# Gate and up products of a decoder trunk: scales read three steps behind POOL's maximum, second buffers for two tiles, the tanh put behind the third copy

## The chip, the cores and the metric

The kernel runs on one core of one Trainium2 chip. The metric is the device time of one execution in microseconds (us), the median of several runs. The profile comes from one more execution, recorded by the hardware profiler. Engines: PE (TensorE, matmuls; PEld is its weight load), DVE (VectorE), ACT (ScalarE), POOL (GpSimd) and SP (SyncE, which here issues the DMAs). Every engine works its instructions off in order.

## What is computed

One layer of a decoder trunk for a prompt of 2048 positions and eight short sequences of four positions: a mixer (pooling and a state space model, gated), then a feed-forward block, then a norm. The change lies in the first half of the feed-forward block:

```python
hn = _rmsnorm(h, norm_ffn[l])
f = jax.nn.silu(jnp.einsum('btd,df->btf', hn, ffn_w_gate[l])) * jnp.einsum('btd,df->btf', hn, ffn_w_up[l])
h = h + jnp.einsum('btf,fd->btd', f, ffn_w_down[l]).astype(h.dtype)
```

`hn` has 2080 rows of 1024, `ffn_w_gate` and `ffn_w_up` are 1024 x 2816, `ffn_w_down` is 2816 x 1024.

## The kernel before, in words

**Blocks and parts.** Gate and up are computed together for blocks of 128 of the 2816 hidden columns: 22 blocks (`NF`). For each block, `up` runs four parts, one for each range `r` of columns of the input (`XR`: 256, 256, 256 and 272 wide), in the order 1, 2, 3, 0. So the first part of a block is `r` = 1, the third (`r` = 3) is the wide one, the fourth is `r` = 0. Blocks 0 to 19 stand in a section whose order on PE, DVE, ACT and POOL is that of the code (`manual_schedule(engines=IN_ORDER)`); what stands ahead of it, the last two blocks and SP's queue are ordered by the scheduler.

**One part.** The two products are made from seven smaller ones (a Strassen-like scheme over two halves of the depth, gate and up). Each small product is 12 matmuls (four depth slices, three combinations of high and low half-precision parts). `part` adds them up in PSUM banks `x`, `y` and `z`, and uses one bank for several partial sums, so PE must wait until ACT has copied a bank out before it adds the next product: `p1` (line 870) is copied after the first product, `p5` (873) after the second, `u` (876) after the third, `v` (882) after the fifth. The order on PE is products 1, 5, 6, 3, 7, 2, 4. DVE forms the up gate's input `g` = `u` + `y` (its tile is called `w1`, `w` in the profile). `gate` is two ACT instructions: a tanh (855) and a scaling (856); the first `gate` writes `t2` (`t` in the profile), the second writes `t1`, whose tile has the name `u`. POOL adds `p5` += `v` (883) and stores `t2` * `p5` (861, and 864 for the 16 additional columns of the third part); DVE adds `p1` += `z`, makes `t1` * `p1` and stores the other half (861).

All temporary tiles come from the pool `ftmp` with one buffer for each name.

**The work between.** Next to the products, the weights of the next block are converted (`prep(i + 1)`): `hi` is ACT's half-precision conversion with a power-of-two scale, `lo` is DVE's remainder, and DVE makes four sums in tiles `cmb`. The weights of the block after that are loaded (`load(i + 2)`: `gr` and `ur`, `wdrow`: a `cmb` tile) and their scales are made (`stat`): DVE reduces the three tiles to maxima, POOL takes the maximum over the 128 partitions (`partition_all_reduce`, line 746), DVE makes the scales from it (749 to 761, in every second block also `pair`, to 772). This side work is a generator; each `yield` ends a step, and `tick` runs one step at each of four places in every part, so a block has 16 steps. Step 1 stands ahead of the first part's products.

**Out of the stage.** `flush` sends a finished pair of ranges to `f_d` by DMA; then `down` follows.

Of the kernel before, what the change touches and what calls it, by code (L numbers as in the profile page):

```python
# [9 lines left out]
F32 = mybir.dt.float32  # L10
# [687 lines left out]
class FFN:  # L698
# [40 lines left out]
    def stat(self, i, d):  # L739

        E, nc = self.E, self.E.nc
        m = E.small.tile([128, 6], F32, tag="fm", name="fm")
        for j, t in enumerate((*(t.rearrange("p k f -> p (k f)") for t in self.R[i]), d)):
            nc.vector.tensor_reduce(m[:, j:j + 1], t, axis=AX.X, op=OP.max, apply_absolute_value=True)
            yield
        nc.gpsimd.partition_all_reduce(m[:, 3:6], m[:, 0:3], 128, RMAX)
        yield
        b = E.small.tile([128, 4], F32, tag="fb", name="fb")
        nc.vector.tensor_copy(b[:, 0:3], m[:, 3:6])
        nc.vector.tensor_scalar(m[:, 0:2], m[:, 3:5], self.kf, None, op0=OP.mult)  # L750
        tt(E, b[:, 3:4], m[:, 0:1], m[:, 1:2], OP.mult)
        s, inv = pow2(E, b, 4, "pf", 2.0 ** -48, 1e18)
        yield

        c = E.small.tile([128, 8], F32, tag="fc", name="fc")
        nc.vector.tensor_scalar(c[:, 0:2], s[:, 0:2], 0.25, None, op0=OP.mult)
        tt(E, c[:, 2:3], s[:, 0:1], inv[:, 1:2], OP.mult)
        nc.vector.tensor_scalar(c[:, 3:4], c[:, 2:3], -1.0, None, op0=OP.mult)
        nc.vector.tensor_scalar(c[:, 6:8], inv[:, 0:2], self.inv_hn, 4.0, op0=OP.mult, op1=OP.mult)
        nc.vector.tensor_scalar(c[:, 4:5], c[:, 6:7], 0.5, None, op0=OP.mult)  # L760
        nc.vector.tensor_scalar(self.st[:, :, i], s[:, 2:4], 0.25, None, op0=OP.mult)
        self.C[i] = c
# [11 lines left out]
    def prep(self, i):  # L774

        E, nc, c = self.E, self.E.nc, self.C[i]
        g, u = self.R.pop(i)
        f = "p k f -> p (k f)"
        a11, a12, a21, a22 = (t[:, k:k + 4].rearrange(f) for t in (g, u) for k in (0, 4))
        W = self.wp.tile([128, 2, 7, 512], F16, name="W")  # L780
        self.W[i] = W
        S = [self.cmb().rearrange("p (j n) -> p j n", j=2) for j in range(2)]
        s1, s2, s3, s4 = (t[:, j] for t in S for j in range(2))
        src = {0: (slice(0, 2), g.rearrange(f), c[:, 0:1]), 3: (slice(3, 5), S[0].rearrange(f), c[:, 1:2]),
               5: (slice(5, 7), S[1].rearrange(f), c[:, 1:2]), 2: (slice(2, 3), a22, c[:, 1:2])}

        def hi(k):
            o, x, s = src[k]
            nc.scalar.activation(W[:, 0, o].rearrange(f), x, AF.Copy, scale=s)

        def lo(k):
            o, x, s = src[k]
            o = [W[:, v, o].rearrange(f) for v in range(2)]
            nc.vector.scalar_tensor_tensor(o[1], x, s, o[0], op0=OP.mult, op1=OP.subtract)

        hi(0)
        tt(E, s1, a21, a22, OP.add)
        nc.vector.scalar_tensor_tensor(s2, a11, c[:, 3:4], s1, op0=OP.mult, op1=OP.add)
        yield
        hi(3)  # L800
        lo(0)
        yield
        nc.vector.scalar_tensor_tensor(s3, a11, c[:, 2:3], a21, op0=OP.mult, op1=OP.subtract)
        nc.vector.scalar_tensor_tensor(s4, a12, c[:, 2:3], s2, op0=OP.mult, op1=OP.subtract)
        hi(2)
        yield
        hi(5)
        lo(3)
        yield
        lo(5)  # L810
        yield
        lo(2)

    def work(self, i):

        yield from self.prep(i + 1)
        if i + 2 < NF:
            self.load(i + 2)
            d = self.wdrow(i + 2)
            yield  # L820
            yield
            yield
            yield
            yield from self.stat(i + 2, d)
            if i % 2:
                self.pair(i + 1)
        yield
# [5 lines left out]
    def part(self, i, r, first):  # L833


        E, nc, tmp = self.E, self.E.nc, self.tmp
        W, c, X = self.W[i], self.C[i], self.X[r]
        w = XR[r][1]
        F = self.F[i % 2][r // 2]
        T = lambda nm: tmp.tile([128, 272], F32, name=nm)[:, :w]  # L840
        bank = lambda: (self.px.tile([128, 512], F32, name="pa", bufs=2) if first else
                        self.ps.tile([128, 512], F32, name="p", bufs=6))[:, :w]

        def mm(q, p, begin, end):
            a, b = self.P[p]
            for k in range(4):
                ka = slice(k * 128, k * 128 + 128)
                for v, (x, y) in enumerate(((0, 0), (0, 1), (1, 0))):
                    nc.tensor.matmul(q, W[:, x, a, ka], X[b][:, y, k, :w], start=begin and k == v == 0,  # L849
                                     stop=end and k == 3 and v == 2, skip_group_check=True)  # L850

        def gate(g, nm):

            t = T(nm)
            nc.scalar.activation(t, g, AF.Tanh, scale=c[:, 4:5])  # L855
            nc.scalar.activation(t, t, AF.Identity, scale=c[:, 5:6], bias=c[:, 5:6])
            return t

        def store(eng, hf, t, u):
            o = (r % 2) * 2  # L860
            eng.tensor_tensor(F[:, o:o + 2, hf], t[:, :256].rearrange("p (b n) -> p b n", b=2),  # L861
                              u[:, :256].rearrange("p (b n) -> p b n", b=2), op=OP.mult)
            if w > 256:
                eng.tensor_tensor(self.fs[:, i, hf], t[:, 256:], u[:, 256:], op=OP.mult)

        p1, p5, u, v, g = (T(x) for x in ("p1", "p5", "u", "v", "w1"))
        x = bank()
        self.tick()
        mm(x, 1, True, False)
        nc.scalar.copy(p1, x)  # L870
        y = bank()
        mm(y, 5, True, False)
        nc.scalar.copy(p5, y)  # L873
        self.tick()
        mm(x, 6, False, False)
        nc.scalar.copy(u, x)
        mm(y, 3, False, True)
        tt(E, g, u, y, OP.add)
        t2 = gate(g, "t2")
        self.tick()  # L880
        mm(x, 7, False, False)
        nc.scalar.copy(v, x)  # L882
        nc.gpsimd.tensor_tensor(p5, v, p5, op=OP.add)  # L883
        tt(E, t2, t2, g, OP.mult)
        store(nc.gpsimd, 1, t2, p5)
        z = bank()
        mm(z, 2, True, True)
        tt(E, p1, p1, z, OP.add)
        t1 = gate(p1, "u")
        self.tick()  # L890
        mm(x, 4, False, True)
        tt(E, t1, t1, p1, OP.mult)
        store(nc.vector, 0, t1, x)
# [6 lines left out]
    def up(self, ctx, cf, X, F):  # L900
# [9 lines left out]
        for j, src in enumerate(self.x_d):  # L910
            t = xp.tile([128, 2, 4, 256], F16, name=f"x0{j}")
            nc.sync.dma_start(t, src)
            X[0].append(t)
        self.load(1)
        self.ps = pool(cf, "fps", 2, space=PSUM)
        n = NF - 2
        with E.tc.manual_schedule(engines=IN_ORDER):
# [792 lines left out]
```

## Time and profile before

| | |
|---|---|
| median of 3 runs | 2493.27 us (2491.67 to 2493.64) |
| the profiled execution's own time | 2488.81 us |
| its span, first to last instruction | 2487.0 us |
| mean granted TensorE clock | 0.981 |
| busy: PE, PEld, DVE, ACT, POOL | 93%, 65%, 67%, 41%, 18% of the span |
| gate and up stage | from about 1120 to 2039 us |

A share of busy time is a mean over stages with different limits; PE at 93% still has idle time, and the rows below say where and for whom it waited. The ends of matmuls are modelled, since they are pipelined: the record of one lasts longer than the distance to the next. So distances between starts are the surer measure.

### The profile page before, as it was taken

What the parts mean: (1) busy time and instruction counts of PE and PEld (TensorE: products, weight loads), DVE (VectorE), ACT (ScalarE), POOL (GpSimd) and SP (SyncE); (2) the same over time, 40 slices, a digit from 0 to 9 for tenths busy, and PEclk for the clock granted to TensorE, in tenths of its full rate; (3) what the DMA queues carried; (4) which work ended last, traced back from release to release, by engine and by line L of the source; (5) the groups of instructions that cost most, each with busy time, mean ns of one, the idle gap of its engine ahead of it and who ended that gap; (6) DMA issues with size and microseconds to landing.
All of it is one profiled execution on the core that took longest, in us unless ns stands there. A gap on an engine that the chain in (4) does not pass through costs nothing. (4 is left out here: it accounts for less than half of the span.)

```text
span 2487.0 us, 43168 instructions
## 1 busy us (share of the span) xinstructions
PE 2303.8 (93%) x16939; PEld 1611.4 (65%) x16939; DVE 1655.2 (67%) x3866; ACT 1020.6 (41%) x1808; POOL 446.0 (18%) x443
## 2 busy tenths in 40 slices
PE   5869999999999999998999999999999899998998
PEld 4745565654578874556878787878788774443443
DVE  7526795747568778786555555455555678789787
ACT  6422332323444424455444444444444453234332
POOL 3300000000000000001222122121212234445342
PEclk9889999999999999999999999999999999999999
DMA  6224234344434453313212122121212244444332
GB/s 219 64 51 115 70 83 104 83 130 165 149 115 124 116 149 140 120 56 120 77 56 73 61 70 74 62 69 60 77 52 77 85 145 152 144 164 153 128 121 76
DMA packets 209777, 258.03 MB, mean 104 GB/s; under 512 B 33046, under 2 KB 170582, under 8 KB 209053
## 3 DMA queue, kind: packets, MB, share of 16 engines
q1 hardware_dynamic: 209397, 254.83, 32.6%
q8 instruction: 132, 2.16, 0.4%
q14 instruction: 72, 0.59, 0.1%
q10 hardware_dynamic: 144, 0.26, 0.0%
q0 software_dynamic: 32, 0.18, 0.0%
HBM read 167.56 MB, written 86.67 MB: 102 GB/s over the span
## 5 line engine op out<-in xcount | busy, mean ns | idle before, releaser
L849 PEld LDWEIGHTS <-W 128*128 128x128 f16 x7392 | 726.4, 98 | 181.3 <-issue 80.5
L849 PE MATMUL p<-m,W 128*128 128x256 f16 (+1 forms) x3084 | 357.0, 275 | 1.9 <-ACT v L882 1.9
L114 PE MATMUL mm<-xl,wh 128*128 128x512 f16 (+4 forms) x1072 | 347.9, 326 | 7.8 <-DVE xl L136 7.8
L113 PE MATMUL mm<-xh,wh 128*128 128x512 f16 (+4 forms) x1072 | 348.4, 326 | 1.7 <-ACT xh L136 1.6
L115 PE MATMUL mm<-xh,wl 128*128 128x512 f16 (+4 forms) x1072 | 347.7, 326 | 1.6 <-DVE wl L53 1.6
L113 PE MATMUL pd<-m,W 128*128 128x512 f16 x616 | 235.5, 382 | 17.8 <-DVE xr L1096 6.5
L849 PE MATMUL p<-x,W 128*128 128x256 f16 x1848 | 210.6, 274 | 30.8 <-ACT v L882 28.2
L849 PE MATMUL p<-xq,W 128*128 128x256 f16 x1764 | 207.2, 276 | 32.0 <-ACT p L873 28.4
L114 PE MATMUL pd<-m,W 128*128 128x512 f16 x616 | 235.4, 382 | 0.0
L115 PE MATMUL pd<-m,W 128*128 128x512 f16 x616 | 234.7, 382 | 0.5 <-DVE W L307 0.5
L883 POOL TENSOR_TENSOR p<-v,p 128x256 f32<-128x256 f32 (+1 forms) x88 | 71.3, 810 | 750.8 <-ACT v L882 604.3
L115 PEld LDWEIGHTS <-wl 128*128 128x128 f16 x1072 | 107.3, 100 | 76.5 <-issue 9.6
L114 PEld LDWEIGHTS <-wh 128*128 128x128 f16 x1072 | 107.1, 100 | 67.6 <-issue 2.6
L113 PEld LDWEIGHTS <-wh 128*128 128x128 f16 x1072 | 107.0, 100 | 64.7 <-issue 0.3
L307 DVE TENSOR_TENSOR w<-u,p 128x272 f32<-128x272 f32 (+1 forms) x86 | 36.3, 422 | 153.6 <-PE p L849 153.6
L1095 POOL TENSOR_TENSOR xq<-xq,xr 128x512 f32<-128x512 f32 x90 | 128.2, 1444 | 40.7 <-DVE xq L1096 16.0
L114 PEld LDWEIGHTS <-W 128*128 128x128 f16 x616 | 60.6, 98 | 92.2 <-issue 22.0
L115 PEld LDWEIGHTS <-W 128*128 128x128 f16 x616 | 60.7, 99 | 74.8 <-issue 2.4
L113 PEld LDWEIGHTS <-W 128*128 128x128 f16 x616 | 60.6, 98 | 73.7 <-issue 2.1
L855 ACT ACTIVATE t<-w,fc 128x256 f32<-128x256 f32 (+1 forms) x88 | 45.0, 511 | 152.3 <-DVE w L307 152.3
L292 ACT ACTIVATE go<-mm,wc 128x512 f32<-128x512 f32 (+1 forms) x80 | 47.6, 603 | 141.4 <-PE mm L115 113.9
L861 POOL TENSOR_TENSOR m<-t,p 128x256 f32<-128x256 f32 x88 | 97.3, 1106 | 9.0 <-POOL p L883 1.1
(472 smaller groups left out, 4440.3 us busy)
## 6 DMA issues: line engine op xcount, KB each, us to landing
f_d<-m SPq DMA_DIRECT2D x44, 512.0 KB, 2.9
xq<-f_d SPq DMA_DIRECT2D x40, 512.0 KB, 4.6
x<-in_x_prompt_dram SPq DMA_DIRECT2D x32, 512.0 KB, 4.7
xq<-h_d SPq DMA_DIRECT2D x32, 512.0 KB, 4.3
g<-g_d SPq DMA_DIRECT2D x56, 256.0 KB, 2.8
g_d<-go SPq DMA_DIRECT2D x48, 256.0 KB, 2.9
gr<-in_ffn_w_gate_dram SPq DMA_DIRECT2D x23, 512.0 KB, 3.9
ur<-in_ffn_w_up_dram SPq DMA_DIRECT2D x23, 512.0 KB, 3.9
```

The lines of the kernel that those rows point to most:

```text
L113: nc.tensor.matmul(q, ah, bh, start=first, stop=False)
L114: nc.tensor.matmul(q, ah, bl, start=False, stop=False)
L115: nc.tensor.matmul(q, al, bh, start=False, stop=last)
L292: nc.scalar.activation(o[:, :w], q[:, :w], AF.Tanh, scale=cc[:, 1:2])
L307: E.nc.vector.tensor_tensor(o, a, b, op=op)
L849: nc.tensor.matmul(q, W[:, x, a, ka], X[b][:, y, k, :w], start=begin and k == v == 0, stop=end and k == 3 and v == 2, skip_group_check=True)
L855: nc.scalar.activation(t, g, AF.Tanh, scale=c[:, 4:5])
L861: eng.tensor_tensor(F[:, o:o + 2, hf], t[:, :256].rearrange("p (b n) -> p b n", b=2), u[:, :256].rearrange("p (b n) -> p b n", b=2), op=OP ...
L883: nc.gpsimd.tensor_tensor(p5, v, p5, op=OP.add)
L1095: add = (lambda o, x: tt(E, o, o, x, OP.add)) if end else (lambda o, x: nc.gpsimd.tensor_tensor(o, o, x, op=OP.add))
```

## The change

It has four parts.

1. In `stat`, two empty steps stand between POOL's maximum and the instructions that read it, so that they come three steps after it and not one. In `prep` and `work` steps move to make room: `load(i + 2)` is issued by `prep` at its fourth step, `lo(2)` moves up to that step and `lo(3)` and `lo(5)` one step back, and an empty step goes. The block still has 16 steps.
2. The tiles `p5` and `t2` come from a new pool `ftm2` with two buffers for each name.
3. The first `gate` (the tanh and scaling that make `t2`) stands behind the copy of `v` and POOL's addition, and `t2` * `g` and POOL's store stand behind the addition of `z`.
4. The load for block 1 is issued in `prep(0)`; the pool `ftm2` is made after the tiles `x0`.

```diff
 def stat(self, i, d):
         nc.gpsimd.partition_all_reduce(m[:, 3:6], m[:, 0:3], 128, RMAX)
         yield
+        yield
+        yield
         b = E.small.tile([128, 4], F32, tag="fb", name="fb")
...
 def prep(self, i):
         hi(2)
         yield
+        lo(2)
         hi(5)
+        if i + 1 < NF:
+            self.load(i + 1)
+        yield
         lo(3)
         yield
         lo(5)
-        yield
-        lo(2)
 
     def work(self, i):
         yield from self.prep(i + 1)
         if i + 2 < NF:
-            self.load(i + 2)
             d = self.wdrow(i + 2)
-            yield
             yield
             yield
             yield
...
 def part(self, i, r, first):
-        T = lambda nm: tmp.tile([128, 272], F32, name=nm)[:, :w]
+        T = lambda nm: (self.tm2 if nm in ("p5", "t2") else tmp).tile([128, 272], F32, name=nm)[:, :w]
...
         tt(E, g, u, y, OP.add)
-        t2 = gate(g, "t2")
         self.tick()
         mm(x, 7, False, False)
         nc.scalar.copy(v, x)
         nc.gpsimd.tensor_tensor(p5, v, p5, op=OP.add)
-        tt(E, t2, t2, g, OP.mult)
-        store(nc.gpsimd, 1, t2, p5)
+        t2 = gate(g, "t2")
         z = bank()
         mm(z, 2, True, True)
         tt(E, p1, p1, z, OP.add)
+        tt(E, t2, t2, g, OP.mult)
+        store(nc.gpsimd, 1, t2, p5)
         t1 = gate(p1, "u")
...
 def up(self, ctx, cf, X, F):
-        self.load(1)
+        self.tm2 = pool(cf, "ftm2", 2)
         self.ps = pool(cf, "fps", 2, space=PSUM)
```

The order on the engines changes with it. (Lines of the changed kernel are one or two higher.) First DVE in the fourth part of a block, from the reading of the maximum (`fb<-fm`); `w` is `g`, `t` is `t2`, `p` is `p1` or a PSUM bank, `fc` and `fst` are the scales. Before:

```order
L749 COPY fb<-fm 128x3
L750 TENSOR_SCALAR fm<-fm,gmf 128x2
L307 TENSOR_TENSOR fb<-fm 128x1
L44 TENSOR_SCALAR pw<-fb 128x4
L45 TENSOR_SCALAR pw<-pw 128x4
L46 TENSOR_SCALAR pw<-pw 128x4
L47 RECIPROCAL pw<-pw 128x4
L307 TENSOR_TENSOR w_12574<-u,p 128x256
L756 TENSOR_SCALAR fc<-pw 128x2
L307 TENSOR_TENSOR fc<-pw 128x1
L758 TENSOR_SCALAR fc<-fc 128x1
```

and with the change:

```order
L307 TENSOR_TENSOR w_12578<-u,p 128x256
L751 COPY fb<-fm 128x3
L752 TENSOR_SCALAR fm<-fm,gmf 128x2
L307 TENSOR_TENSOR fb<-fm 128x1
L44 TENSOR_SCALAR pw<-fb 128x4
L45 TENSOR_SCALAR pw<-pw 128x4
L46 TENSOR_SCALAR pw<-pw 128x4
L47 RECIPROCAL pw<-pw 128x4
L307 TENSOR_TENSOR p_12574<-p_12574,p 128x256
L307 TENSOR_TENSOR t_12656<-t_12656,w_12578 128x256
L758 TENSOR_SCALAR fc<-pw 128x2
```

`g` stood behind the seven instructions that read the maximum, and now stands ahead of them; the product with `t` and the addition to `p` now stand ahead of the scales `fc`, with the addition first.

Second, ACT in the first part of a block, from the first conversion (`W<-gr`, step 1) to the second `gate`. Before:

```order
L789 ACTIVATE W<-gr,fc 128x1024
L870 COPY p_13183<-p 128x256
L873 COPY p_13184<-p 128x256
L789 ACTIVATE W<-cmb,fc 128x1024
L876 COPY u<-p 128x256
L855 ACTIVATE t_13250<-w_13187,fc 128x256
L856 ACTIVATE t_13250<-t_13250,fc 128x256
L789 ACTIVATE W<-ur,fc 128x512
L882 COPY v<-p 128x256
L855 ACTIVATE u<-p_13183,fc 128x256
L856 ACTIVATE u<-u,fc 128x256
```

and with the change:

```order
L791 ACTIVATE W<-gr,fc 128x1024
L872 COPY p_13186<-p 128x256
L875 COPY p_13187<-p 128x256
L791 ACTIVATE W<-cmb,fc 128x1024
L878 COPY u<-p 128x256
L791 ACTIVATE W<-ur,fc 128x512
L883 COPY v<-p 128x256
L857 ACTIVATE t_13270<-w_13190,fc 128x256
L858 ACTIVATE t_13270<-t_13270,fc 128x256
L857 ACTIVATE u<-p_13186,fc 128x256
L858 ACTIVATE u<-u,fc 128x256
```

The copy of `v` stood behind the tanh and scaling of `t`, and now stands ahead of them; the conversion `W<-ur` of step 3 now follows the copy of `u`.

Third, ACT where the gate and up stage begins: `p<-pa` are the copies of `p1` and `p5` in the very first part, `tp` are transposes of the last rows of the stage ahead, which `L1534` (`L1536`) copies out. Before:

```order
L870 COPY p_12215<-pa 128x256
L873 COPY p_12216<-pa 128x256
L789 ACTIVATE W<-cmb,fc 128x1024
L876 COPY u<-pa 128x256
L52 ACTIVATE hi<-x,shn 128x512
L855 ACTIVATE t_12282<-w_12219,fc 128x256
L856 ACTIVATE t_12282<-t_12282,fc 128x256
L789 ACTIVATE W<-ur,fc 128x512
L1534 COPY m<-tp 128x8x128
```

and with the change:

```order
L872 COPY p_12218<-pa 128x256
L52 ACTIVATE hi<-x,shn 128x512
L1536 COPY m<-tp 128x8x128
L52 ACTIVATE hi<-T,shn 128x1536
L52 ACTIVATE hi<-x,shn 128x512
L1536 COPY m<-tp 128x8x128
L1536 COPY xr_11770<-tp 128x8x128
L1536 COPY xr_11771<-tp 128x8x128
L875 COPY p_12219<-pa 128x256
L791 ACTIVATE W<-cmb,fc 128x1024
```

The second copy, `p5`, followed `p1` at once; with the change it comes after the last conversions and copies of the stage ahead.

## Rows read from the trace of the kernel before

**Rows 1.** The page: busy time and share of the span of PE, and the clock that was granted to it in 40 equal slices of the span (tenths of full speed).

```profile
PE 2303.8 (93%) x16939; PEld 1611.4 (65%) x16939; DVE 1655.2 (67%) x3866; ACT 1020.6 (41%) x1808; POOL 446.0 (18%) x443
...
PEclk9889999999999999999999999999999999999999
```

**Rows 2.** Who kept PE waiting from 1156 to 1965 us: in total, times, longest.

```profile
PE p L849 <- ACT p L873: 28.4, 19, 2.3
PE p L849 <- ACT v L882: 28.2, 20, 1.9
```

**Rows 3.** PE in order of time in the gate and up stage: start, duration, instruction, count, and in brackets the idle time before it and what ended it. Fourth part of block 0, second and third part of a block from 1510.99, the fourth from 1529.89, the fourth of block 19, and the first part after it.

```profile
1175.96 1.47 PE L849 MATMUL p<-x,W 128*128 128x256 f16 x12 [1.43 <-ACT v L882]
...
1510.99 12.11 PE L849 MATMUL p<-m,W 128*128 128x256 f16 x108
...
1529.89 8.02 PE L849 MATMUL p<-x,W 128*128 128x256 f16 x72
...
1945.69 1.47 PE L849 MATMUL p<-x,W 128*128 128x256 f16 x12 [1.14 <-ACT v L882]
...
1952.62 5.21 PE L849 MATMUL p<-xq,W 128*128 128x256 f16 x31 [2.30 <-ACT p L873]
```

**Rows 4.** All engines in order of time in the second part of a block, whose first matmul starts at 1430.84.

```profile
1430.84 10.72 PE L849 MATMUL p<-m,W 128*128 128x256 f16 x96
...
1434.96 0.37 ACT L876 COPY u<-p 128x256 f32<-128x256 f32 x1 [0.88 <-PE p L849]
1436.35 0.42 DVE L307 TENSOR_TENSOR w<-u,p 128x256 f32<-128x256 f32 x1 [1.68 <-PE p L849]
1436.80 0.51 ACT L855 ACTIVATE t<-w,fc 128x256 f32<-128x256 f32 x1 [1.46 <-DVE w L307]
...
1437.85 0.35 ACT L882 COPY v<-p 128x256 f32<-128x256 f32 x1
...
1438.89 0.42 DVE L307 TENSOR_TENSOR p<-p,p 128x256 f32<-128x256 f32 x1 [0.44 <-PE p L849]
...
1439.35 0.51 ACT L855 ACTIVATE u<-p,fc 128x256 f32<-128x256 f32 x1 [1.15 <-DVE p L307]
...
1440.53 0.42 DVE L307 TENSOR_TENSOR u<-u,p 128x256 f32<-128x256 f32 x1 [1.21 <-ACT u L856]
1441.04 0.42 DVE L861 TENSOR_TENSOR m<-u,p 128x256 f32<-128x256 f32 x1
```

**Rows 5.** All engines in order of time, from the end of a third part (POOL's `fs`) through the fourth, whose first matmul starts at 1449.73, into the first part of the next block.

```profile
1449.41 0.22 POOL L864 TENSOR_TENSOR fs<-t,p 128x16 f32<-128x16 f32 x1
...
1449.73 8.02 PE L849 MATMUL p<-x,W 128*128 128x256 f16 x72
...
1455.77 0.38 POOL L746 PARTITION_ALL_REDUCE fm<-fm  x1 [6.14 <-issue]
...
1457.78 0.42 DVE L307 TENSOR_TENSOR w<-u,p 128x256 f32<-128x256 f32 x1 [0.27 <-PE p L849]
1458.12 0.16 DVE L756 TENSOR_SCALAR fc<-pw 128x2 f32<-128x2 f32 x1
...
1459.22 0.34 DVE L772 SCALAR_TENSOR_TENSOR fc<-fc,fst 128x1 f32<-128x1 f32 x2
1459.28 0.35 ACT L882 COPY v<-p 128x256 f32<-128x256 f32 x1
...
1459.68 1.47 PE L849 MATMUL p<-x,W 128*128 128x256 f16 x12 [1.92 <-ACT v L882]
...
1462.30 0.69 DVE L307 TENSOR_TENSOR cmb<-ur 128x512 f32<-128x512 f32 x1
...
1462.84 0.73 POOL L883 TENSOR_TENSOR p<-v,p 128x256 f32<-128x256 f32 x1 [6.68 <-ACT W L789]
1463.02 1.09 DVE L798 SCALAR_TENSOR_TENSOR cmb<-gr,fc,cmb 128x512 f32<-128x512 f32 x1
1463.64 1.05 POOL L861 TENSOR_TENSOR m<-t,p 128x256 f32<-128x256 f32 x1
1464.04 1.74 DVE L794 SCALAR_TENSOR_TENSOR W<-gr,fc,W 128x1024 f16<-128x1024 f32 x1
1464.73 0.37 ACT L873 COPY p<-p 128x256 f32<-128x256 f32 x1 [1.86 <-POOL m L861]
1465.00 1.15 ACT L789 ACTIVATE W<-cmb,fc 128x1024 f16<-128x1024 f32 x1
```

**Rows 6.** Who waited for whom from 1156 to 1965 us, two rows on the maximum over partitions: in total, times, longest. "issue" is time that nothing in the trace explains.

```profile
POOL fm L746 <- issue: 119.5, 20, 6.5
...
DVE fb L749 <- POOL fm L746: 95.1, 20, 5.3
```

**Rows 7.** All engines in order of time where the stage begins: the last split of the rows ahead of it (`lo<-T`), a product of the first part, the last copies of transposes (`xr<-tp`), and the first matmuls of the third part.

```profile
1141.38 1.81 DVE L53 SCALAR_TENSOR_TENSOR lo<-T,shn,hi 128x1536 f16<-128x1536 f32 x1
...
1142.01 2.74 PE L849 MATMUL pa<-xq,W 128*128 128x256 f16 x12
...
1146.97 1.90 ACT L1534 COPY xr<-tp 128x1024 f16<-128x1024 f16 x2
...
1156.78 0.63 PE L849 MATMUL p<-m,W 128*128 128x272 f16 x4
```

**Rows 8.** The same place as a window: its length, busy time and count of PE, PEld, DVE, ACT and POOL, the granted clock, DMA share and GB/s.

```profile
1141.00:1145.00 4.00, 3.82 (x28) 3.07 (x29) 3.85 (x5) 0.38 (x2) 3.45 (x2) 0.57 0.46 131
```

## The prediction

> **What bounds the kernel now.** First the page: TensorE (PE) is busy 93% of the span, at a granted clock of 0.9 or more in every slice from the fourth on [rows 1]; so time is won only where PE stands still. Next, who kept PE waiting in the gate and up stage (1156 to 1965 us): two copies of ScalarE (ACT), line 882 (`v`) 20 times for 28.2 us and line 873 (`p5`) 19 times for 28.4 us [rows 2]. Then PE in order of time [rows 3]: the wait on `v` comes in the fourth part of each block, the wait on `p5` in the first part of the next.
>
> The size of both, from starts of matmuls alone: 72 matmuls of 256 columns take 8.02 us and 12 take 1.47, so 60 take 6.55, 0.1092 each, 1.31 a product and 9.17 a part. Second and third part run without a wait from 1510.99 to 1529.89, 18.90 us. A block without waits would be 18.90 + 2 x 9.17 = 37.24 us. From 1175.96 to 1945.69 there are 19 blocks of 40.51, so 3.27 is lost in each, 62.1 in all; the first `v` wait (1.43) and the last `p5` wait (2.30) lie outside it: 65.8 us. The wait rows name 56.6; they count from a modelled matmul end, which lies behind the next matmul's slot. I take 63 as what these two waits cost, with 57 and 66 as bounds.
>
> What causes them [rows 4, 5]. In an undisturbed part (start 1430.84) VectorE (DVE) forms `g` at +5.51, ACT takes the tanh at +5.96 and copies `v` at +7.01 to +7.36, half a microsecond before PE's seventh product needs it (six products, +7.86). In the fourth part (start 1449.73) DVE stands in its queue before the scales: POOL is done with the third part at 1449.63, but the maximum over partitions only starts 6.14 us later, ends at 1456.15, and the scales come before `g`: `g` is at 1457.78, +8.05, 2.5 us late, and tanh, `v` and PE (1459.68) with it. After the maximum POOL does nothing for 6.68 us more, so its pair of this part, line 883 and the store 861, ends at 1464.69. The next part's `p5` copy follows at 1464.73: it has one buffer and the store reads it. Over the stage the 6 us ahead of the maximum stand 20 times (119.5 us, ended by nothing that the trace names), and DVE's wait behind them for 95.1 us [rows 6].
>
> **The change part by part.**
>
> *Second buffers for `p5` and `t2`.* The first part's `p5` goes into the buffer that the third part left before the maximum. The `p5` wait goes: about half of the 63.
>
> *`v` ahead of the tanh.* Five products are done at +6.55; copies stand some 0.2 behind their product (`u`, after three products of 3.93, at +4.12). So `v` is at +6.74 to +7.09 and the seventh product finds it 0.77 early, no matter when `g` comes. The tanh moves to +7.1 and its second half ends near +8.3 (tanh to product takes 1.18, from +8.51 to +9.69), while `z`, which ACT and DVE wait for anyway, is added at +8.05. Nothing for a plain part; in the fourth the `v` wait goes, the other half.
>
> *The scales three steps later.* The reductions and the maximum move one step forward, the reading two steps back, behind `g` (the order of DVE in the fourth part). When does the maximum come? The third part's store now follows `z`'s addition: that is about +8.55 there (1/16 more columns), 0.43 long, the product with `g` as long, then POOL's store and its 16-column piece, 0.73 (as line 883) and 0.22: +10.4 of a part of 9.73, so 0.7 into the fourth part, where it was done 0.1 before it. With 5.97 + 0.38 the maximum is there at +7.05. The first scales took 1.36 (1456.15 to 1457.51, the 0.27 idle before `g`): DVE is at +8.4 where `z` wanted +8.05. `z` and the product with `g` go to +9.3, then the second scales, 1.44 (1458.12 to 1459.56) in odd blocks and an estimated 0.6 less in even ones, which have no `pair`. The product `t1*p1`, +9.69 in a plain part, is at +10.1 or +10.75; DVE's last two end at +11.0 or +11.7, 1.85 or 2.5 into the next part. Behind them stand the two sums for the conversion of `S[0]` (0.69 and, before beside POOL, 1.09; 0.75 is my estimate without POOL): 3.3 or 3.95. ACT's conversion of 1.15 follows, then `u`, copied by 4.85 or 5.5 where PE's fifth product wants it at 5.24. Even blocks lose nothing, odd ones about 0.3 to 0.5; I take 0.25 a block, 5 us in all. ACT's first conversion of the next block now needs scales written at +9.5, and ACT is free at +10.2 anyway. Bounds: 0, and 1.2 a block (24 us) if this conversion waits for the last scale and every step is as slow as the slowest row.
>
> *Loads.* `gr` and `ur` are asked for at the fourth step instead of the sixth; `ur` is released earlier because `lo(2)` moves ahead, `lo(3)` and `lo(5)` one step back onto DVE time that is idle in a plain second part. They are read at the ninth step, more than a part later. On SP's queue they stand behind the previous block's store to `f_d`, which waits for POOL's late pair, 6 into the first part; `gr` is free after that only. Cost nothing.
>
> *The start.* Order moved here too: the first `p5` copy of ACT stands behind the last transposed copies of the stage before, and PE can do three products, not seven, before them. DVE's last split there ended at 1141.38 + 1.81 = 1143.2, ACT's last two copies at 1146.97 + 1.90 = 1148.9 [rows 7]; with four of the part's instructions out of their way I put the `p5` copy near 1147. Four products (5.24) and a part (9.17) later PE is at 1161.4, where it was at 1156.78: 4.6 late. [...]
>
> *The last two blocks* are ordered by the scheduler; apart from the `p5` wait counted above I leave them as they are.
>
> **Sum.** -63 + 5 + 6 = -52. The profiled execution took 2488.8 (span 2487.0); it gives 2436.8. The median of the runs, 2493.3, lies 4.5 above the profiled execution: **2441 us**.
>
> **Rivals.**
>
> *The scales become the bound.* Every microsecond by which the maximum comes after +6.7 passes through `z`, the tanh, `t1*p1` and the two sums to ACT's `u`, and there is no slack left in odd blocks. With 1.2 to 2.4 lost per block instead of 0.25 the time is 2460 to 2484. For it: POOL starts on the maximum only when its own store is done, later than now. Against it: the longest of the 20 gaps is 6.5, half a microsecond over the mean [rows 6].
>
> *Slower: `v` waits for POOL.* `v` keeps one buffer, and POOL's line 883 of the fourth part reads it. After the maximum POOL does nothing for 6.68: 883 starts at +13.7, 4.6 into the next part, and ends at 5.3; the next `v` copy can wait until 7.5 without cost. If it ended later than 7.5 + 63/20 = 10.6, the gain would be gone; at 12, 4.5 a block are lost, 90 us: about 2525. For it: POOL's late pair now falls on DVE's `lo(0)`, which took 1.74 beside it, and on the next sums. Against: 883 itself took 0.73 there [rows 5]. [...]
>
> *The `p5` wait stays*, because it was ACT's place in its queue and not the buffer: 63/2 is won, about 2472. Against: the copy starts 0.04 after the store's end [rows 5].
>
> *Nothing changes*, the waits only move: 2488 to 2498.
>
> **How the numbers follow.** Forecast 0.72, own range 2427 (66 won, nothing lost) to 2466 (63 won, 24 and 12 lost); scales as bound 0.12; `p5` stays 0.06; nothing 0.03; slower 0.07. The range 2426 to 2474 holds the forecast, `p5` and the nearer half of the scales' case. A difference of 0.2%, 5 us, is about what runs of this kernel can tell from none. Faster: 0.72 + 0.12 + 0.06 = 0.90; same 0.03; slower 0.07.
>
> **What would show it.** Right: blocks of 37.3 to 37.8 us in PE's starts; no wait of PE on `v` in the fourth and on `p5` in the first part; `g` of the fourth part ahead of the scales, the wait on the maximum a microsecond instead of 5; POOL's late pair still late, with nobody behind it; PE's first 272-column product after 1159. Wrong: PE waiting on `u` or `p1` in each first part (scales), on `v` there (POOL), or blocks still near 40.

## The result, and the profile after

| | before | after |
|---|---|---|
| median of the runs, us | 2492.47 (4 runs, 2488.58 to 2493.64) | 2433.01 (4 runs, 2431.53 to 2434.37) |
| the profiled execution's own time, us | 2488.81 | 2434.37 |
| its span, us | 2487.0 | 2432.2 |
| mean granted clock | 0.981 | 0.977 |

The ratio is 0.9766, with a 95% interval of 0.9751 to 0.9782: 59 us faster. The forecast was 2441, with a range of 2426 to 2474.

The rows below answer to those of before. First the page, PE and its clock, as in [rows 1]:

```profile
PE 2298.3 (94%) x16939; PEld 1613.6 (66%) x16939; DVE 1641.4 (67%) x3866; ACT 1021.6 (42%) x1808; POOL 425.8 (18%) x443
PEclk9889999999999999998999999999999999999999
```

Who kept PE waiting from 1150 to 1975 us, as in [rows 2] (in total, times, longest):

```profile
PE p L851 <- ACT p L872: 6.3, 3, 3.1
PE p L851 <- ACT v L883: 2.8, 3, 1.4
PE pa L851 <- ACT p L875: 1.4, 1, 1.4
```

In the loop, from block 1 to block 19, the waits on `v` and `p5` (now line 875) are gone. What is left lies in the first parts of block 0 (`pa` banks) and in the last two blocks. PE in order of time, from the fourth part of one block into the block after the next, as in [rows 3]:

```profile
1437.50 9.33 PE L851 MATMUL p<-x,W 128*128 128x256 f16 x84
1446.67 9.33 PE L851 MATMUL p<-xq,W 128*128 128x256 f16 x84
1455.84 12.11 PE L851 MATMUL p<-m,W 128*128 128x256 f16 x108
...
1474.74 9.33 PE L851 MATMUL p<-x,W 128*128 128x256 f16 x84
1483.91 9.33 PE L851 MATMUL p<-xq,W 128*128 128x256 f16 x84
```

From fourth part to fourth part it is 37.24 us, what the forecast worked out for a block without waits. Over all blocks, from the last 272-column rows of block 0 (1174.04) to those of block 19 (1881.91), it is 37.26. By the same rows before had 40.53 (1163.73 to 1933.75).

All engines in the fourth part and the beginning of the next block, as in [rows 4, 5]:

```profile
1437.92 0.22 POOL L866 TENSOR_TENSOR fs<-t,p 128x16 f32<-128x16 f32 x1
...
1443.01 0.42 DVE L307 TENSOR_TENSOR w<-u,p 128x256 f32<-128x256 f32 x1 [3.96 <-PE p L851]
1444.01 0.38 POOL L746 PARTITION_ALL_REDUCE fm<-fm  x1 [5.87 <-issue]
1444.30 0.37 ACT L883 COPY v<-p 128x256 f32<-128x256 f32 x1 [2.30 <-PE p L851]
...
1447.42 0.34 DVE L774 SCALAR_TENSOR_TENSOR fc<-fc,fst 128x1 f32<-128x1 f32 x2
1447.68 0.42 DVE L307 TENSOR_TENSOR u<-u,p 128x256 f32<-128x256 f32 x1
...
1448.54 0.68 DVE L307 TENSOR_TENSOR cmb<-ur 128x512 f32<-128x512 f32 x1
1449.26 0.75 DVE L800 SCALAR_TENSOR_TENSOR cmb<-gr,fc,cmb 128x512 f32<-128x512 f32 x1
...
1451.10 0.35 ACT L878 COPY u<-p 128x256 f32<-128x256 f32 x1
...
1451.71 0.72 POOL L884 TENSOR_TENSOR p<-v,p 128x256 f32<-128x256 f32 x1 [7.31 <-ACT u L878]
...
1452.51 0.72 POOL L863 TENSOR_TENSOR m<-t,p 128x256 f32<-128x256 f32 x1
...
1453.47 0.38 ACT L883 COPY v<-p 128x256 f32<-128x256 f32 x1 [1.39 <-PE p L851]
```

`g` is at +5.51 even here, the maximum ends at +6.89, `v` is copied at +6.80, and `u` of the next first part at +4.43. PE's fifth product wants this copy done at +5.24, and it takes 0.35, so it is 0.46 early. POOL's late pair ends 15.1 after the third part's `fs` (1438.14 to 1453.23), as it did before (1449.63 to 1464.69), and now nobody stands behind it. The two waits of [rows 6], from 1150 to 1975 us:

```profile
DVE fb L751 <- POOL fm L746: 22.9, 20, 1.7
...
POOL fm L746 <- issue: 120.5, 20, 6.6
```

POOL's 6 us ahead of the maximum are untouched; DVE's wait behind them fell from 95.1 to 22.9.

The stage's beginning, as in [rows 7, 8]: ACT's first `p1` copy, the last copies of transposes, the first `p5` copy, then PE's next products, and a window just ahead of them, with a granted clock of 0.50.

```profile
1132.87 0.38 ACT L872 COPY p<-pa 128x256 f32<-128x256 f32 x1
...
1147.92 1.93 ACT L1536 COPY xr<-tp 128x1024 f16<-128x1024 f16 x2 [1.10 <-PE tp L1535]
1149.73 0.39 ACT L875 COPY p<-pa 128x256 f32<-128x256 f32 x1
...
1150.17 7.47 PE L851 MATMUL pa<-xq,W 128*128 128x256 f16 x48 [1.44 <-ACT p L875]
...
1167.09 2.94 PE L851 MATMUL p<-m,W 128*128 128x272 f16 x24
...
1141.00:1150.00 9.00, 3.93 (x32) 3.35 (x33) 3.44 (x4) 5.95 (x8) 0.00 (x0) 0.50 0.81 291
```

The budget of the span, -54.8:

| stretch | before | after | difference |
|---|---|---|---|
| up to the stage's first product | 1120.4 | 1122.7 | +2.3 |
| from there to the first 272-column product | 36.4 | 44.4 | +8.0 |
| from there to the start of block 20 | 790.2 | 726.8 | -63.4 |
| last two blocks | 92.0 | 87.8 | -4.2 |
| down stage and end | 448.0 | 450.6 | +2.6 |

### The profile page after: what moved, and what is told of

The parts are those of the page before. It is cut to its first block, busy times and chain, and to the rows that moved or that the text cites. A ratio compares the mean times of both kernels' runs of the same rounds, so it can differ in the third digit from the quotient of the medians.

```text
span 2432.2 us, 43171 instructions
## 1 busy us (share of the span) xinstructions
PE 2298.3 (94%) x16939; PEld 1613.6 (66%) x16939; DVE 1641.4 (67%) x3866; ACT 1021.6 (42%) x1808; POOL 425.8 (18%) x443
## 5 line engine op out<-in xcount | busy, mean ns | idle before, releaser
L851 PE MATMUL p<-xq,W 128*128 128x256 f16 x1764 | 198.4, 274 | 4.8 <-ACT p L872 3.5
L883 ACT COPY v<-p 128x272 f32<-128x272 f32 (+1 forms) x86 | 32.2, 375 | 165.1 <-PE p L851 162.7
L113 PE MATMUL po<-woh,m 128*128 128x512 f16 x256 | 97.0, 379 | 0.9 <-DVE x L307 0.9
```

What stands on the lines that cost most here:

```text
L113: nc.tensor.matmul(q, ah, bh, start=first, stop=False)
```

## The experiments

"Before" in the ratios of the experiments is the kernel before, run beside them (2489.1 to 2489.4); the first and the eighth row are those of the section above. "Block" is the mean distance between the last 272-column rows of block 0 and block 19, over 19; "start" is from the stage's first product to the first 272-column product of the profiled execution.

| kernel | median, us | ratio (95%) | block | start |
|---|---|---|---|---|
| before | 2492.47 | 1 | 40.53 | 36.4 |
| buffers alone | 2465.43 | 0.9902 (0.9888 to 0.9917) | 38.97 | 44.2 |
| tanh alone | 2500.51 | 1.0039 (1.0026 to 1.0053) | 41.40 | 35.4 |
| scales alone | 2481.31 | 0.9958 (0.9940 to 0.9976) | 40.22 | 36.6 |
| tanh and scales | 2501.74 | 1.0050 (1.0034 to 1.0067) | 41.39 | 36.6 |
| buffers and scales | 2434.11 | 0.9782 (0.9768 to 0.9797) | 37.40 | 43.8 |
| buffers and tanh | 2449.02 | 0.9840 (0.9826 to 0.9855) | 38.01 | 46.4 |
| all (after) | 2433.01 | 0.9766 (0.9751 to 0.9782) | 37.26 | 44.4 |
| all, second buffer for `p5` alone | 2432.23 | 0.9773 (0.9759 to 0.9788) | 37.24 | 45.8 |
| all, old tiles at the start | 2421.74 | 0.9725 (0.9712 to 0.9739) | 37.24 | 36.7 |
| scales, `p5`'s buffer, old tile at the start | 2427.20 | 0.9749 (0.9735 to 0.9764) | 37.52 | 36.1 |
| scales, late pair on VectorE | 2426.80 | 0.9753 (0.9736 to 0.9769) | 37.41 | 36.2 |

### Each part alone

**Buffers alone**: the pool `ftm2`, nothing else.

```diff
-        T = lambda nm: tmp.tile([128, 272], F32, name=nm)[:, :w]
+        T = lambda nm: (self.tm2 if nm in ("p5", "t2") else tmp).tile([128, 272], F32, name=nm)[:, :w]
...
+        self.tm2 = pool(cf, "ftm2", 2)
```

> The kernel before with the second buffers for p5 and t2 alone; the scales and the tanh stay where they were. My theory: PE loses 3.27 us in each block at two places, half on v in the fourth part (g stands behind the scales) and half on p5 in the next first part (its one buffer is still read by POOL's late store). This run takes only the p5 half away: blocks of 38.8 to 38.9 us instead of 40.51, no p5 wait in PE's rows, the v waits still there with some 28 us, the start about 8 us later as in the changed kernel; so some 23 us less than before, 2468 to 2472. Rival (the place of the p5 copy in ACT's queue holds it, not the buffer): the p5 waits stay and the time is that of before or 8 above it. Rival (the start is late because of the moved loads, not of the new tiles): the p5 half is won in full, about 2461.

Measured: 2465.4, the start 44.2. In PE's waits from 1150 to 1975 us `p5` is gone from the loop and `v` unchanged (its longest two rows):

```profile
PE p L849 <- ACT v L882: 28.2, 21, 1.9
PE p L849 <- ACT p L870: 4.7, 3, 3.4
```

Blocks fell by 1.56, 29.6 us in 19. My theory held here, and the start's loss came with the tiles: this kernel has none of the moved loads.

**Tanh alone**: the first `gate` behind the `v` copy.

```diff
         tt(E, g, u, y, OP.add)
-        t2 = gate(g, "t2")
...
         nc.gpsimd.tensor_tensor(p5, v, p5, op=OP.add)
-        tt(E, t2, t2, g, OP.mult)
-        store(nc.gpsimd, 1, t2, p5)
+        t2 = gate(g, "t2")
...
         tt(E, p1, p1, z, OP.add)
+        tt(E, t2, t2, g, OP.mult)
+        store(nc.gpsimd, 1, t2, p5)
```

> The kernel before with the tanh put behind the v copy alone; one buffer for all tiles, scales where they were. My theory: v no longer waits for g, so PE's wait on v in the fourth part goes; but g, tanh and t2 are as late as before, POOL's late pair too, and p5 of the next first part still waits for POOL's store: blocks near 38.9 us, the p5 waits still there, v gone, the start as before: about 31 us less than before, 2459 to 2465. Rival (g is still 2.5 us late, so the product t1*p1 and the sums for the next conversion come later and PE waits on u or p1 in the next first part instead): less than 10 us won, 2483 or more.

Measured: 2500.5, slower than before. PE's waits from 1150 to 1975 us:

```profile
PE p L849 <- ACT p L873: 48.9, 20, 2.9
PE p L849 <- ACT p L870: 16.4, 20, 1.5
PE p L849 <- ACT v L881: 1.1, 1, 1.1
```

`v` went as expected (28.2 to 1.1), but `p5` grew from 28.4 to 48.9, and `p1` came new with 16.4. The theory that each wait has a price of its own fell. The wait on `p1` is the one that the rival named.

**Scales alone**: the two empty steps in `stat`, the moved loads and splits.

```diff
         nc.gpsimd.partition_all_reduce(m[:, 3:6], m[:, 0:3], 128, RMAX)
         yield
+        yield
+        yield
...
+        lo(2)
         hi(5)
+        if i + 1 < NF:
+            self.load(i + 1)
...
```

> The kernel before with the reading of the scales three steps after the maximum and the moved loads and splits alone; one buffer for all tiles, the tanh ahead of v. My theory: g of the fourth part no longer stands behind the maximum, so v finds it in time without any move of the tanh: the v wait goes, the p5 wait stays: blocks near 38.9 us, about 31 us less than before (2459 to 2465); so for v this part and the tanh's move would each do alone. The start is as before if the new tiles make it late, 8 us later if the moved loads do (2467 to 2473). Rival (the late scales cost what my forecast put as a bound, 1.2 us a block): 24 us of it given back, 2483 to 2489.

Measured: 2481.3, with runs from 2470.2 to 2487.4. The rows: PE's waits, then PE in order of time in one first part, then two windows, the first over the wait and the second behind it.

```profile
PE p L851 <- ACT p L875: 43.3, 20, 2.9
...
PE p L851 <- ACT v L884: 0.2, 1, 0.2
...
1455.76 4.09 PE L851 MATMUL p<-xq,W 128*128 128x256 f16 x36
1462.21 7.07 PE L851 MATMUL p<-xq,W 128*128 128x256 f16 x48 [2.35 <-ACT p L875]
...
1455.00:1462.00 7.00, 4.86 (x45) 4.21 (x43) 4.61 (x16) 2.72 (x5) 1.44 (x2) 1.00 0.00 0
1462.00:1469.00 7.00, 6.79 (x47) 5.46 (x47) 3.11 (x6) 4.07 (x9) 1.45 (x2) 0.76 0.42 134
```

Again `v` is gone and `p5` has taken it over (43.3). Behind this wait the granted clock is 0.76, where it was 1.00 in the 7 us before: the 48 matmuls take 7.07 where they took 5.56 in the block ahead (from 1422.29, at a granted clock of 1.00), 1.5 us more. By the starts of matmuls this happened in 7 of blocks 1 to 19, 10.0 us in all; the clock was read in two of them and was 0.76 in both. The mean granted clock of the runs goes with their times: 0.979 at 2470.2, 0.974 at 2487.4.

**What the two misses say.** In [rows 5] PE and POOL both run from the third part's `v` to the next first part's third product, side by side. POOL has its pair, 6 us of nothing, the maximum, 7 us of nothing and the late pair. PE has two products, the fourth part with its wait on `v`, and three products. They meet at the `p5` copy, and what PE loses on `v` ahead of that it doesn't lose on `p5` any more. So the `v` wait of before lay in the shadow of the `p5` wait. From the `p5` copy PE works on to the third part's `v`, and the ring is closed; with one buffer it sets the block. Behind the longer waits on `p5` the matmuls also ran slower: 10.0 us with the scales alone, 9.4 in 6 blocks with the tanh alone, nothing in the kernel before, whose waits on `p5` were 1.8 at most in the loop.

### The ring

**All but the buffers** (tanh and scales):

> The changed kernel without the second buffers: the late scales and the moved tanh together, one buffer for every tile. New theory, after the first runs: with one buffer for p5 a block closes a ring through POOL (the third part's v, POOL's pair, the 6 us ahead of the maximum, the 7 us after it, the fourth part's late pair, the p5 copy of the next first part, and PE's work from there to the third part's v again). This ring is some 40 to 42 us long whether or not PE also waits for v; so without the buffers nothing is won: blocks of 40 to 42 us, a p5 wait of 2 to 3.5 in each, 2475 to 2505. My old theory (each of the two waits costs its own 31 us and can be removed alone): blocks near 38.9, 2459 to 2465.

Measured: 2501.7, 13 us slower than before; PE's waits, then POOL in order of time over one turn of the ring:

```profile
PE p L851 <- ACT p L875: 59.3, 20, 4.1
...
1449.76 0.76 POOL L884 TENSOR_TENSOR p<-v,p 128x272 f32<-128x272 f32 x1 [7.17 <-ACT v L883]
...
1458.34 0.39 POOL L746 PARTITION_ALL_REDUCE fm<-fm  x1 [5.87 <-issue]
1465.74 0.71 POOL L884 TENSOR_TENSOR p<-v,p 128x256 f32<-128x256 f32 x1 [7.02 <-DVE W L796]
1466.53 0.72 POOL L863 TENSOR_TENSOR m<-t,p 128x256 f32<-128x256 f32 x1
...
1491.47 0.76 POOL L884 TENSOR_TENSOR p<-v,p 128x272 f32<-128x272 f32 x1 [7.17 <-ACT v L883]
```

From the third part's addition to the end of the maximum it is 8.97, to the late store's end 8.52 more, and to the next third part's addition 24.22: 41.71. The same turn in the kernel before, around [rows 5]:

```profile
1447.89 0.76 POOL L883 TENSOR_TENSOR p<-v,p 128x272 f32<-128x272 f32 x1 [8.02 <-ACT v L882]
...
1487.61 0.76 POOL L883 TENSOR_TENSOR p<-v,p 128x272 f32<-128x272 f32 x1 [8.02 <-ACT v L882]
```

There the three pieces were 8.26, 8.54 and 22.92: 39.72, the shortest turn of that kernel. Over the 18 turns from the third part of block 1 to that of block 19 the means are 8.11, 9.50 and 22.91 before, and 9.05, 8.75 and 23.59 here. The 0.9 more ahead of the maximum is the store, which now waits for `t2` * `g` behind `z`. The way back is 22.91 to 22.92 in every turn before: PE does the same work each time, with no wait on POOL in it. Here it is 22.54 in seven turns and 23.84 to 25.29 in eleven. In these the matmuls behind the wait on `p5` ran slower; in the turn shown the 48 took 7.07 behind a wait of 2.64, at a granted clock of 0.75, and in the turn ahead of it 5.40 behind one of 2.46, at 1.00.

Without these slower stretches the ring is 40.3, no longer than the 40.5 of before. In 12 blocks they cost 20.6 us, more than the 16.5 by which the profiled execution is longer than that of before. So without the buffers the ring still sets the block, nothing is won, and what is lost lies in the slower matmuls. Against the scales alone, whose ring is 39.7 without such stretches (means of 8.12 and 8.62, and a way back of 22.91), the moved tanh makes it 0.7 longer. The new theory held for the ring, though it had no slower matmuls in it; the old one asked for 2459 to 2465.

**The ring cut at another place**: scales alone, and in the fourth part VectorE does what POOL did late; one buffer everywhere.

```diff
-        nc.gpsimd.tensor_tensor(p5, v, p5, op=OP.add)
+        (nc.vector if r == 0 else nc.gpsimd).tensor_tensor(p5, v, p5, op=OP.add)
...
-        store(nc.gpsimd, 1, t2, p5)
+        store(nc.vector if r == 0 else nc.gpsimd, 1, t2, p5)
```

> The kernel with the late scales alone (one buffer for every tile, the tanh ahead of v), but in the fourth part of each block VectorE makes the addition to p5 and the store that POOL made late. If the ring through POOL is what holds p5, cutting it at this place does what the second buffer did: the p5 copy of the next first part need not wait for POOL, blocks of 37.3 to 37.7 (VectorE is 0.8 later with the sums for the first conversions, which costs up to 0.4 in odd blocks), 2421 to 2432. If something else held p5 (ACT's queue, PE's bank), the p5 waits of 2 to 3 stay: 2470 to 2490.

Measured: 2426.8, blocks of 37.41, and no wait on `p5` from 1150 to 2000 us:

```profile
PE p L851 <- ACT p L872: 8.7, 5, 3.4
PE p L851 <- ACT v L884: 2.8, 2, 2.0
```

The tile still has one buffer, and only the engine of 44 instructions changed against the kernel with the scales alone: 54.5 us less, some 10 of them the slower matmuls behind the waits on `p5`, which no longer come. So it was POOL's late pair that held `p5`, and a second buffer is one of two ways out.

### Which part does what once `p5` is free

**Tanh back** (buffers and scales):

> The changed kernel with the tanh back ahead of the v copy: late scales and second buffers remain. Theory: with the scales behind g the tanh is ready in time, and PE waits on v no more than with the tanh moved (the kernel with the late scales alone had next to no v wait): blocks of 37.24 to 37.4 us, 2430 to 2437, no difference from the changed kernel that a run can tell. Rival (the tanh's move is needed, because z, the scales or the late pair push g back in the fourth part): a v wait of 0.3 to 1.4 in each block, 2438 to 2462.

**Scales back** (buffers and tanh):

> The kernel before with the second buffers and the moved tanh, the scales where they were. By my forecast's first theory this has all the gain and even saves the cost of the late scales: v does not wait for g, p5 has its buffer: blocks of 37.24, 2430 to 2436. Rival, from the run with the tanh alone, where PE waited for the p1 copy 20 times for 16.4 us: g, then z, t1*p1 and the sums come late because DVE waits for the maximum ahead of them, ACT's conversion for the next block holds the p1 and u copies of the first part, and PE waits there: 0.8 to 1.6 lost in each block, 2447 to 2466.

**One second buffer** (all, but `t2` from the old pool):

```diff
-        T = lambda nm: (self.tm2 if nm in ("p5", "t2") else tmp).tile([128, 272], F32, name=nm)[:, :w]
+        T = lambda nm: (self.tm2 if nm == "p5" else tmp).tile([128, 272], F32, name=nm)[:, :w]
```

> The changed kernel with a second buffer for p5 alone; t2 has one again. Theory: t2 of the first part is written by the tanh after the v copy, at about 7 us of the part, and POOL's late store that reads the old one ends about 6 us into it; so t2's second buffer does nothing: 2430 to 2437, blocks of 37.24. Rival (the late store ends after the tanh's turn in some blocks, ACT stands still and the v or p1 copy behind it is late): some 0.5 to 1 lost in a block, 2441 to 2453.

Tanh back: 2434.1, against 2433.0 no difference; blocks are 0.14 longer. The seventh product of each first part starts some 0.17 late, since the copy of `v` stands behind the tanh there and ends at +7.98, where it is wanted at +7.86 (9.50 in this row, 9.33 in those of the section on the result):

```profile
1444.05 9.50 PE L851 MATMUL p<-xq,W 128*128 128x256 f16 x84
```

Scales back: 2449.0, 16 us worse, and the wait is on `p1`, alternately long and short (1.38, then 0.22 in the next block):

```profile
PE p L849 <- ACT p L870: 14.8, 19, 3.1
...
1456.80 6.71 PE L849 MATMUL p<-xq,W 128*128 128x256 f16 x60 [1.38 <-ACT p L870]
```

So with `p5` free it is the scales' move that takes the `v` wait away (38.97 to 37.40 a block); the loads and splits that moved with the scales weren't tried apart. The tanh's move does 0.96 of the same 1.57 when it is alone. Then `g` is still late (+8.71 in the fourth part ahead of the row above), and ACT's two `gate`s and its first conversion stand behind it and ahead of the next block's `p1` copy, which comes at 1456.40. `t2`'s second buffer does nothing beside the moved tanh: 2432.2, 37.24.

### The start

**Old tiles at the start** (all, but the two parts that run with the `pa` banks take `p5` and `t2` from the old pool):

```diff
-        T = lambda nm: (self.tm2 if nm in ("p5", "t2") else tmp).tile([128, 272], F32, name=nm)[:, :w]
+        T = lambda nm: (self.tm2 if nm in ("p5", "t2") and not first else tmp).tile([128, 272], F32, name=nm)[:, :w]
```

> The changed kernel, but the parts that run ahead of the others at the start take p5 and t2 from the old pool and not from the new one, so that the first p5 copy need not wait for the memory in which the new tiles lie. My theory: the 8 us that the start lost come from that copy standing behind the last transposed copies of the stage before; with the old tiles PE can do seven products there again as before, and the first 272-column product comes some 36 to 38 us after the stage's start instead of 44: 2425 to 2427 against 2433 of the changed kernel. Rival (the start is late because of the order of the loads or of ACT's queue, whatever the tile): no difference, 2431 to 2435.

Measured: 2421.7, the fastest of all. ACT's first two copies, and PE's first 272-column product:

```profile
1128.69 0.38 ACT L872 COPY p<-pa 128x256 f32<-128x256 f32 x1
1128.96 0.39 ACT L875 COPY p<-pa 128x256 f32<-128x256 f32 x1
...
1155.25 2.94 PE L851 MATMUL p<-m,W 128*128 128x272 f16 x24
```

`p5` is copied 0.27 after `p1`, where it was 16.86 after it, and the start takes 36.7 again. Against the changed kernel the span is 13.3 us shorter: 7.7 at the start, 1.6 in the loop and the last blocks, and 4.2 ahead of the stage. For these last I have no cause; the stage's first product lies between 1118.5 and 1122.7 in all the kernels. In the table every kernel that takes `p5` from the new pool in these parts starts in 43.8 to 46.4, every other in 35.4 to 36.7; `p5` alone is enough (45.8). What about the new pool puts the copy late in ACT's order (the memory it lies in, or when it comes free) wasn't tried apart.

**The least change** (the scales, and `p5` alone from the new pool, not in those first parts; tanh and `t2` as before):

> The kernel before with only what the runs so far ask for: the scales three steps behind the maximum (with the moved loads and splits) and a second buffer for p5 alone, which the parts that run ahead of the others at the start don't use; the tanh stays ahead of the v copy, t2 has one buffer. Theory: the moved tanh and t2's second buffer do nothing here, and the old tile saves the 8 us at the start: blocks of 37.24 to 37.3, the first 272-column product some 36 us after the stage's start, 2419 to 2425, as with all four changes and the old tile at the start. Rival (the tanh's move and t2's buffer each have a slack in which the other one's absence is hidden, and without both PE waits on v or p1): 0.3 or more in each block, 2428 or more.

Measured: 2427.2, between the theory's upper end and the rival's lower; blocks of 37.52, 0.28 more than with everything. Where it goes, ACT in a first part that starts at 1436.65:

```profile
1443.73 0.71 ACT L791 ACTIVATE W<-ur,fc 128x512 f16<-128x512 f32 x1
...
1444.34 0.35 ACT L884 COPY v<-p 128x256 f32<-128x256 f32 x1
```

The tanh, its scaling and a conversion stand ahead of `v`, which is copied at +7.69 to +8.04, where PE's seventh product wanted it at +7.86. In the changed kernel the same copy stood at +6.80 to +7.18 (1453.47, in the rows of the section on the result; the part starts at 1446.67). So the moved tanh does have a use, in the first part. The 0.28 x 19 = 5.3 us, of the 5.5 between the two medians, are not all its own: with two buffers for `t2` the tanh ahead of `v` cost 0.16 a block (tanh back, 37.40, against 37.24), 3.1 us. The other 2.2 come with `t2`'s one buffer, which counts only when the tanh stands ahead of `v`: the tanh starts at +6.03 instead of +5.97, and in three blocks at +6.30 to +6.50, behind POOL's late store. So each of the two hid what the other was worth, as the rival had it.

## Why the prediction was right, and where it was not

**What bounds, and the size.** Right: blocks of 37.3 to 37.8 us were named, and 37.26 came, at their lower end. The two waits were put at 63, the last one, 2.30 in block 20, among them. The loop gave 63.4 without that one, so 65.7 with it: the bound that came from the starts of matmuls (65.8), while the 56.6 of the wait rows, which I let pull the value down, was too little. Among the 65.7 is a third wait that the forecast hadn't named, on the copy of `v` in each first part: the seventh product started 1.48 behind the sixth and not 1.31, 3.2 us in 19 blocks.

**Half and half, wrong as causes.** "About half of the 63" held for the buffers: 29.6. "In the fourth the `v` wait goes, the other half", put down to the tanh, is the step that failed. The tanh alone lost 11 us; next to the buffers it gave 18 (0.96 x 19), and next to buffers and scales 2.7 (0.14 x 19). The scales do this half (1.57 x 19 = 30 next to the buffers). I had costed them at a loss of 5 and given them no gain. The forecast priced the two waits as if they stood one after the other, and they stand side by side. That the sum came out right in spite of this is luck: all three parts were in the change. The halves can't be had one by one, since without the buffers none of the rest wins more than 8 between medians.

**The late scales.** +5 was predicted, and PE shows no wait in the loop; by the starts of matmuls two blocks are longer than 37.24, by 0.04 and 0.28, both at the fifth product, which wants `u`. The maximum was forecast at +7.05 and came at +6.89. The tight place was the right one: in odd blocks (this one, with `pair`) the `u` copy was to end at 5.5 where the limit is 5.24, and it ended at 4.78. What was too dear is the stretch between the scales and `t1*p1`: I put this product at +10.75 in such blocks, and it was at 1447.68, +10.18. The small instructions start before the records ahead of them end (the last scales at 1447.42 are recorded for 0.34, and the product starts 0.26 after them).

**The start.** +6 predicted, +8.0 measured. `p5` was put near 1147, 26.6 after the stage's first product; it came 27.0 after it (1149.73 - 1122.71). That is 0.4 of the 2.0 that were missing. Another 0.4 lie between the start of the copy and PE's next product (1150.17), for which no time was taken. Of the 6 in the sum, 4.6 is worked out from the rows; the rest, 1.3 and rounded up, was an estimate from the 12 matmuls at 1142.01 in [rows 7], 2.74 long and not 1.47 as in [rows 3], and no run shows the 6 or its upper bound of 12. In place of the 1.3 the trace showed 2.1, the 0.8 that was still missing: the granted clock was 0.50 in the 9 us before, in which PE was busy for 3.93, and 0.68 from 1150 to 1157, and the 48 matmuls took 7.31 from start to start instead of 5.24. The last 0.4 were lost in the second part, where PE waited for a store of DVE (9.61 from 1157.48 to 1167.09, and not 9.17). Behind the waits on `p5` in the kernels with one buffer the length of the wait doesn't tell: with tanh and scales the 48 matmuls took 7.07 behind one of 2.43 and 5.40 behind one of 2.90.

**The last two blocks**, left at nothing beyond the `p5` wait of 2.30, gave 4.2, so 1.9 more; the kernel with the buffers alone already has it (87.3 us from block 20 to the down stage, 92.0 before). What lies outside the stage, ahead of it and behind, took 4.9 back; no term was named for it, and no experiment was on it. So part of the agreement is errors that cancel: the waits gave 2.7 more than the 63, the scales cost 5 less and the last blocks gave 1.9 more, against 2.0 more at the start and these 4.9.

**From the profile to the median.** Profile to profile it is 54.4, against 52. The rest of the miss, 5.9 of 8.3 (the forecast was 2441.3 before rounding), is the median's place: it was taken 4.5 above the profiled execution, as before the change, and came 1.4 below it.

**The rivals.** The scales as the bound: no. `v` waiting for POOL: the late addition ends 5.76 into the next block where 5.3 was forecast, the `v` copy comes at 6.80. (Its price was summed wrongly: 90 on top of 2441 are 2531, not 2525.) `p5` held by ACT's queue: the buffers alone and the pair on VectorE both exclude it.

## What to carry to other kernels

Two waits in one block can stand side by side and not one after the other: before a price is put on one, follow both chains to the point where they meet, since removing the shorter one may give nothing (here from 8 us less to 13 more) and removing the longer one leaves the other. A ring that goes through one engine and comes back into a tile with one buffer can set the period, as the one through POOL did here (39.72 us at its shortest, in blocks of 40.53); another buffer cut it (37.40 beside the scales), and so did moving the late reader to another engine (37.41). A new pool can cost at a place that the diff doesn't touch: the first copy into its tile stood late in ACT's order, at the start, and using the old tile there gave 8 us back. And what one part of a change is worth depends on the others: the moved tanh lost 11 us alone, gave 18 beside the buffers and 3 beside buffers and scales.

## What the runs showed of the hardware

- Behind a wait of PE the matmuls ran slower in some blocks. In the three kernels with one buffer and longer waits on `p5` (tanh, scales, both), the 48 matmuls behind this wait took 1.25 to 2.75 us longer in 25 of 57 blocks, behind waits of 1.95 to 3.60 us; in the three blocks in which it was read the granted clock behind it was 0.76, 0.76 and 0.75. In the other 32 blocks, behind waits of 1.80 to 2.94, they took no longer than without such a wait; in three of them the 48 took 5.56, 5.40 and 5.40 behind waits of 2.28, 2.26 and 2.46, at a granted clock of 1.00. So how long PE had waited doesn't settle it, and what does stays open.
- The 6 us ahead of POOL's maximum (5.9 to 6.1 on the mean in each of the twelve kernels) and the 7 us from it to POOL's next instruction (7.02 and 7.31 in the rows above) stayed, whatever stood around them; only with the pair on VectorE, where POOL's next work came later, did 11 us pass behind it. So around one maximum of 0.38 POOL did nothing else for some 13 us of each block.
